# Rest of the modulation, first gelu and first layer norm beside the last gates instead of in the merge

## The chip, the cores and the metric

The kernel runs on one core of a Trainium2 chip. The metric is device time in microseconds of one execution. A core has TensorE (matrix products, an in-order queue of its own), VectorE, ScalarE and GpSimd, each with an in-order queue, and SyncE, which here issues most DMAs. TensorE's granted clock has the levels 1.2 and 2.4 GHz; the profile gives it as a share, 1.00 being the higher one.

## The reference

One layer of a hybrid backbone over 2048 latent tokens of 1024 channels with 256 context tokens. Cut to what the change touches:

```python
mod_l = silu_c @ ada_w + ada_b              # 1024 -> 6*1024, one row
sh1, sc1, g1, sh2, sc2, g2 = split(mod_l, 6)
zl = modulate(rmsnorm(x, norm1_g), sh1, sc1) @ w_in   # 512 | 1024 | 2048 columns
g  = gelu(s5_mixer(zl[:, :512]))
ya = (g * sigmoid(g @ w_glu)) @ w_a
yb = silu(layernorm(depthwise_conv1d(glu(zl[:, 512:1536])))) @ w_b
x  = x + g1 * ((sigmoid(ga) * ya + sigmoid(gb) * yb) @ w_out)   # ga, gb: zl[:, 1536:]
nl = modulate(rmsnorm(x, norm2_g), sh2, sc2)
x  = x + g2 * conv_ffn(nl)
```

Only `sh1` and `sc1` are needed for the first projection. The other four parts, `g1`, `sh2`, `sc2` and `g2` (4096 columns of `ada_w`), are needed after the merge.

## The kernel before, in words

Tokens lie on the free axis, in four blocks b = 0 to 3 of 512; channels lie on the 128 partitions. Each fp32 product is emulated by three matmuls of high and low halves (`mm3`, L462 to L464), so a 128-column tile of the projection with K = 1024 takes 24 matmuls of 128x512 for a block.

Order of the stages: a first phase (norm, modulation, the projection's S5 columns, the GLU columns), then 16 gate columns `gate(m)`, four blocks each, whose sigmoids (L859) go to DRAM. Beside the gate blocks `background()` advances two generators, the S5 scan and the depthwise convolution, both written to DRAM (`d_y`, `d_cv`). Gates m = 14 and 15 come last, in `last_gates`: block 3 of both, then blocks 0 to 2 of m = 14, then of m = 15.

The merge (`phase3a`) then runs over four blocks. In each it does 48 matmuls with `w_glu` on the gelu of the S5 output (`gh`, `go`), 96 with `w_b` on the layer-normed convolution (`sln`) and 96 with `w_a` (on `tgl`), multiplies by the stored gates and stores `mg`. While block b runs, `gelu_block(b + 1)` and `ln_block(b + 1)` prepare the next one. Gelu and layer norm of block 0 are emitted between the two halves of the last gates. The layer norm takes two sums over the channels by matmuls with ones: the mean (L977), after which the values are centred (L980) and squared, and the variance (L988), after which come L990 (variance), a square root on ScalarE, a reciprocal (L992), the products L993 to L996 and the product with the values (L998). The output is scaled and split into halves (L449 on ScalarE, L453 on VectorE).

The rest of the modulation (`ada_rest`) is a generator that the merge advances once per column m. For eight groups j of 512 columns and eight tiles k of 128 rows it loads 256 KB of `ada_w` (L924) into one of two slabs and adds it, times silu(c), to one of two accumulators (k = 0 by L926, the others by L928). `collect(j)` then sums the accumulator over the partitions: groups 0, 1, 6 and 7 (`g1`, `g2`) by one matmul L907 into a row, to which a bias row loaded into the tile `adrow` is added and which is stored to `d_row`; groups 2 to 5 (`sh2`, `sc2`) by four matmuls L913 into columns. In the text c0 to c7 are these collects.

A tile scheduler sets the order of each engine's queue from the program order and the priorities; `urgent()` raises that of the gates' sigmoids. Tiles come from pools: `z8` (8 buffers), `t16` (6), `raw` (3 landing buffers for weights), and two groups of PSUM tiles of four. Weight halves are loaded to `raw` and split by ScalarE (L449) and VectorE (L453).

Of the kernel before, what the change touches and what calls it, by code (L numbers as in the profile page):

```python
# [9 lines left out]
F32 = mybir.dt.float32  # L10
F32R = mybir.dt.float32r
# [12 lines left out]
T = 8  # L24
# [406 lines left out]
class Net:  # L431
# [6 lines left out]
    def __init__(self, nc, tc, ins, out):  # L438
        self.nc, self.tc, self.ins, self.out = nc, tc, ins, out
        self.v, self.a, self.g, self.pe = nc.vector, nc.scalar, nc.gpsimd, nc.tensor  # L440
        self.dma = nc.sync.dma_start
        self.store = nc.scalar.dma_start
        self.low = "g"


    def split(self, hi, lo, src, ha="a", la="v"):
# [150 lines left out]
    def phase1(self):  # L597
        nc, tc, ins, scr, v, a = self.nc, self.tc, self.ins, self.scr, self.v, self.a
        w_in = ins["w_in"]
        with ExitStack() as ctx:  # L600
# [152 lines left out]
            cvp = rx.enter_context(self.pool("cvp", 2, side="right"))  # L753
            fill = []

            stage = []

            def s5_all():
                yield from tabs
# [45 lines left out]
                    yield  # L805

            pace = [0.0, 0.0]

            def background(nconv=None, ns5=None):
# [80 lines left out]
            self.phase3a(last_gates(), lx, psum)  # L890


    def ada_rest(self, psum, fp):

        v, cp, pe = self.v, self.cp, self.pe
        self.A2 = cp.tile([128, 8], F32, name="A2")
# [4 lines left out]
        def collect(j, acc):  # L901
# [34 lines left out]
        v.scalar_tensor_tensor(self.A2, self.A2, 1.0, self.col["n2"], op0=OP.add, op1=OP.mult)  # L936
        yield

    def phase3a(self, last_gates, lx, psum):
        nc, tc, ins, scr, v, a, g_ = self.nc, self.tc, self.ins, self.scr, self.v, self.a, self.g  # L940
        with ExitStack() as ctx:
            fp = ctx.enter_context(self.pool("f3", 1, side="right"))
# [5 lines left out]
            def gelu_block(b):  # L948
                yr = self.z8("yr", [128, 4, T, 64])
                for ct in range(4):  # L950
                    self.dma(yr[:, ct], scr["y"][8 * ct:8 * ct + 8, :, :, 64 * b:64 * b + 64]
                             .rearrange("g h s c -> (g h) s c"))
                gl = self.z8("gl", [128, 4, 512])
                for ct in range(4):
                    a.activation(gl[:, ct].rearrange("p (c s) -> p c s", s=T),
                                 yr[:, ct].rearrange("p s c -> p c s"), AF.Gelu_apprx_tanh)
                gh = self.z8("gh", [128, 4, 512], F32R)
                go = self.z8("go", [128, 4, 512], F32R)
                for ct in range(4):
                    self.split(gh[:, ct], go[:, ct], gl[:, ct], "a", "v")  # L960
                return gl, gh, go

            def ln_block(b, out):

                t512 = lambda nm: fp.tile([128, 512], F32, name=nm, tag="ln", bufs=4)
                cv = self.z8("cv", [128, 4, 512])
                cb = lambda ct: self.col["cb"][:, ct:ct + 1]
                nb = 512 // CS
                for ct in range(4):
                    self.dma(cv[:, ct].rearrange("p (s x) -> p s x", s=CS), scr["cv"][ct][:, :, nb * b:nb * b + nb])  # L970
                s1, s2 = t512("s1"), t512("s2")
                v.scalar_tensor_tensor(s1, cv[:, 0], cb(0), cv[:, 1], op0=OP.add, op1=OP.add)
                v.scalar_tensor_tensor(s2, cv[:, 2], cb(2), cv[:, 3], op0=OP.add, op1=OP.add)
                v.scalar_tensor_tensor(s1, s1, self.cb13, s2, op0=OP.add, op1=OP.add)
                yield
                pm = psum.tile([128, 512], F32, name="ps", tag="ax")
                self.pe.matmul(pm, self.ones, s1, start=True, stop=True)  # L977
                a.activation(s2, pm, AF.Copy, scale=1.0 / D_CONV)
                for ct in range(4):
                    v.scalar_tensor_tensor(cv[:, ct], cv[:, ct], cb(ct), s2, op0=OP.add, op1=OP.subtract)  # L980
                q1, q2 = t512("q1"), t512("q2")
                a.activation(q1, cv[:, 0], AF.Square)
                for ct in range(1, 4):
                    a.activation(q2, cv[:, ct], AF.Square)
                    v.tensor_tensor(q1, q1, q2, op=OP.add)
                yield
                pv = psum.tile([128, 512], F32, name="ps", tag="ax")
                self.pe.matmul(pv, self.ones, q1, start=True, stop=True)  # L988
                va, sd, rs = t512("va"), t512("sd"), t512("rs")
                v.tensor_scalar(va, pv, 1.0 / D_CONV, EPS, op0=OP.mult, op1=OP.add)  # L990
                a.activation(sd, va, AF.Sqrt)
                v.reciprocal(rs, sd)  # L992
                v.tensor_tensor(sd, rs, rs, op=OP.mult)  # L993
                v.tensor_tensor(sd, sd, va, op=OP.mult)
                v.tensor_scalar(sd, sd, -0.5, 1.5, op0=OP.mult, op1=OP.add)
                v.tensor_tensor(rs, rs, sd, op=OP.mult)  # L996
                for ct in range(4):
                    v.tensor_tensor(cv[:, ct], cv[:, ct], rs, op=OP.mult)  # L998
                yield
                s = self.t16("sln", [128, 2, 4, 512])  # L1000
                out.append(s)
                for ct in range(4):
                    a.activation(cv[:, ct], cv[:, ct], AF.Silu, bias=self.col["lb"][:, ct:ct + 1],
                                 scale=self.col["lg"][:, ct:ct + 1])
                    nat = lambda z: z.rearrange("p (x s) -> p x s", s=CS)
                    self.split(nat(s[:, 0, ct]), nat(s[:, 1, ct]), cv[:, ct].rearrange("p (s x) -> p x s", s=CS), "a", "v")

            self.cb13 = self.cp.tile([128, 1], F32, name="cb13")
            v.tensor_tensor(self.cb13, self.col["cb"][:, 1:2], self.col["cb"][:, 3:4], op=OP.add)
            sq = []  # L1010
            next(last_gates)
            gnext = gelu_block(0)
            for _ in ln_block(0, sq):
                pass
            for _ in last_gates:
                pass
            lx.close()
            gp = ctx.enter_context(self.pool("g3", 3))
            wab = {}
            for nm, src in (("b", ins["w_b"]), ("a", ins["w_a"])):  # L1020
                for k2 in range(2):
                    wab[nm, k2] = self.t16(f"w{nm}{k2}", [128, 2, 2, 1024])
                for k in range(4):
                    for hf in range(2):
# [5 lines left out]
            self.wo = {}  # L1030
            for b in range(4):
                bs = slice(512 * b, 512 * b + 512)
                gl, gh, go = gnext
# [30 lines left out]
                for m in range(10):  # L1064
                    if m < 8:
                        wb(m)
                    if m == 1 and b < 3:
                        gnext = gelu_block(b + 1)
                    if m >= 2:
                        wa(m - 2)  # L1070
                    if m == 3 and b < 3:
                        ln = ln_block(b + 1, sq)
# [5 lines left out]
            for _ in ada:  # L1078
                pass


    def phase3b_4(self):
# [329 lines left out]
```

## Time and profile before

| | |
|---|---|
| median of 3 runs | 2810.7 us (2806.5 to 2811.0) |
| profiled execution | 2806.18 us, span 2804.4 us |
| TensorE busy | 2711.9 us, 97% of the span |
| VectorE busy | 1508.0 us, 54% |
| ScalarE busy | 822.7 us, 29% |
| gates 13 to 15 in the trace | 815.2 to 884.7 us |
| merge in the trace | 884.7 to 1147.7 us |

The span is the time from the first to the last instruction in the trace; the execution's own time is 1.8 us longer. In the rows PE is TensorE, PEld its weight loads, DVE VectorE, ACT ScalarE, POOL GpSimd, SP SyncE. "x2" behind a row means two instructions taken together, and a bracket behind a row gives the idle time of the engine before it and what ended it. Matmuls overlap with the next one, so a steady row of 0.39 us stands for a step of about 0.23 us from one start to the next.

### The profile page before, as it was taken

To read this page: it belongs to the slowest core of one execution; us is meant where nothing else is said; L and a number is where in the kernel's file an instruction comes from. 1 tells how busy PE (TensorE), PEld (TensorE's weight loads), DVE (VectorE), ACT (ScalarE), POOL (GpSimd) and SP (SyncE) were. 2 spreads that over 40 slices of the span, in tenths; PEclk is the share of its full clock that TensorE was granted. 3 is DMA by queue.
4 is the path that set the end of the run, shared out by engine and by line. 5 is a ranking of instruction groups with operands and counts; after the bars stand their busy time and mean duration, and the time that the engine had idled before them with its cause. 6 is when DMAs were issued, how large, how long until landed. Compare 5 with 4: busy or idle time off the path is not lost.

```text
span 2804.4 us, 32119 instructions
## 1 busy us (share of the span) xinstructions
PE 2711.9 (97%) x12044; PEld 2203.2 (79%) x12044; DVE 1508.0 (54%) x2312; ACT 822.7 (29%) x1446; POOL 459.3 (16%) x504
## 2 busy tenths in 40 slices
PE   7998999999999999999999999999999989999998
PEld 3786878788887777788888888888888878787887
DVE  5867643433316788566855646556465462414154
ACT  2555412121235443243421222212222132212122
POOL 2256477667600000000000000000000000000000
PEclk8999999999999999999999999999999999999999
DMA  8645745354436576533111111111111153323143
GB/s 315 195 142 165 205 138 153 126 177 147 145 102 202 173 206 200 187 131 113 64 46 57 42 49 49 49 53 46 45 57 42 53 179 107 113 71 135 53 143 98
DMA packets 327308, 334.73 MB, mean 119 GB/s; under 512 B 95336, under 2 KB 240360, under 8 KB 324464
## 3 DMA queue, kind: packets, MB, share of 16 engines
q1 hardware_dynamic: 245680, 235.13, 27.2%
q10 hardware_dynamic: 81472, 97.54, 10.0%
q8 instruction: 95, 1.56, 0.2%
q14 instruction: 61, 0.50, 0.1%
HBM read 230.38 MB, written 102.21 MB: 119 GB/s over the span
## 4 chain that ended last, share of the span: by engine, by line
PE 75%; DVE 9%; DMA 6%; POOL 5%; issue 2%; ACT 2%; SPq 0%; ACTq 0%; POOLq 0%; DVEq 0%
PE ps L464 23%; PE ps L462 23%; PE ps L463 23%; DMA sgab<-d_sg 2%; PE ps L795 1%; DVE Hs L408 1%; PE ps L577 1%; PE ps L385 1%; POOL t L395 1%; DVE Hs L410 1%; DMA slab<-in_ada_w_dram 1%; DMA ada<-in_ada_w_dram 1%; POOL t L394 1%; POOL t L361 1%; PE ps L1112 0%
## 5 line engine op out<-in xcount | busy, mean ns | idle before, releaser
L1242 DVE SCALAR_TENSOR_TENSOR acc<-pad,fw,acc 128x1024 f32<-128x1024 f32 x352 | 450.4, 1282 | 238.9 <-ACT acc L1238 229.5
L477 POOL TENSOR_TENSOR rs_y<-rs_v,mhalf 128x1 f32<-128x1 f32 (+1 forms) x41 | 27.4, 668 | 2048.8 <-DVE rs_v L476 2048.8
L462 PE MATMUL ps<-wd,hhl 128*128 128x512 f32 x704 | 275.6, 393 | 13.5 <-ACT hhl L449 7.3
L463 PE MATMUL ps<-wd,hhl 128*128 128x512 f32 x704 | 275.7, 392 | 0.0
L464 PE MATMUL ps<-wd,hhl 128*128 128x512 f32 x704 | 275.3, 392 | 0.1
L408 DVE TENSOR_TENSOR_SCAN Hs<-m,S 64x287 f32<-64x287 f32 x64 | 68.8, 1075 | 240.5 <-POOL S L396 240.1
L453 DVE TENSOR_TENSOR hhl<-hr,hhl 128x512 fp32r<-128x512 f32 (+1 forms) x110 | 63.0, 582 | 244.4 <-ACT hhl L449 244.1
L453 DVE TENSOR_TENSOR w_ch<-w_raw,w_ch 128x512 fp32r<-128x512 f32 x134 | 106.4, 801 | 137.9 <-ACT w_ch L449 137.5
L462 PEld LDWEIGHTS ps<-wd,hhl 128*128 128x128 f32 x704 | 133.2, 189 | 43.3 <-ACT hhl L449 7.9
L449 ACT CAST w_ch<-w_raw 128x512 fp32r<-128x512 f32 x142 | 87.6, 621 | 267.2 <-PE ps L464 167.1
L463 PEld LDWEIGHTS ps<-wd,hhl 128*128 128x128 f32 x704 | 133.2, 189 | 28.6 <-DVE wd L453 1.0
L464 PEld LDWEIGHTS ps<-wd,hhl 128*128 128x128 f32 x704 | 133.1, 189 | 28.5 <-DVE hhl L453 0.8
L449 ACT CAST hhl<-hr 128x512 fp32r<-128x512 f32 (+1 forms) x110 | 57.2, 534 | 264.5 <-PE ps L464 231.3
L463 PE MATMUL ps<-nm2l,w_ch 128*128 128x512 f32 x344 | 133.8, 389 | 0.0
L464 PE MATMUL ps<-nm2h,w_ch 128*128 128x512 f32 x344 | 133.8, 389 | 0.0
L462 PE MATMUL ps<-nm0h,w_ch 128*128 128x512 f32 x344 | 133.8, 389 | 0.0
L463 PE MATMUL ps<-nm0l,w_ch 128*128 128x512 f32 x344 | 133.8, 389 | 0.0
L463 PE MATMUL ps<-nm1l,w_ch 128*128 128x512 f32 x344 | 133.8, 389 | 0.0
L463 PE MATMUL ps<-nm3l,w_ch 128*128 128x512 f32 x344 | 133.8, 389 | 0.0
L464 PE MATMUL ps<-nm0h,w_ch 128*128 128x512 f32 x344 | 133.8, 389 | 0.0
L462 PE MATMUL ps<-nm1h,w_ch 128*128 128x512 f32 x344 | 133.8, 389 | 0.0
L464 PE MATMUL ps<-nm1h,w_ch 128*128 128x512 f32 x344 | 133.8, 389 | 0.0
(370 smaller groups left out, 6354.5 us busy)
## 6 DMA issues: line engine op xcount, KB each, us to landing
w_raw<-in_ffn_w_up_dram SPq DMA_DIRECT2D x88, 256.0 KB
d_hid<-acc ACTq DMA_DIRECT2D x88, 256.0 KB
w_raw<-in_ffn_w_down_dram SPq DMA_DIRECT2D x76, 256.0 KB
grp<-d_rec SPq DMA_DIRECT2D x32, 576.0 KB
hr<-d_hid SPq DMA_DIRECT2D x66, 256.0 KB
d_sg<-sgg ACTq DMA_DIRECT2D x64, 256.0 KB
ada<-in_ada_w_dram SPq DMA_DIRECT2D x64, 256.0 KB
sgab<-d_sg SPq DMA_DIRECT2D x32, 512.0 KB
```

The lines of the kernel that those rows point to most:

```text
L361: g_.tensor_tensor(r1, Hl, tb[:, 0:1, LAT].to_broadcast([128, 2, NCL]), op=OP.mult)
L385: nc.tensor.matmul(ps[:, :NX], sm[:, i, :], ug, start=True, stop=True)
L394: g_.tensor_tensor(t1, S, tb[:, 0:1, :].to_broadcast([128, 2, NX]), op=OP.mult)
L395: g_.tensor_tensor(t2, S[:, ::-1, :], tb[:, 1:2, :].to_broadcast([128, 2, NX]), op=OP.mult)
L408: v.tensor_tensor_scan(Hs[0:64, i, 1:1 + nsc], mb[0:64], S[0:64, i, 0:nsc], 0.0, op0=OP.mult, op1=OP.add)
L410: v.tensor_tensor_scan(Hs[64:128, i, NX - 1 - nsc:NX - 1][:, ::-1], mb[64:128], S[64:128, i, NX - nsc:NX][:, ::-1], 0.0, op0=OP.mult, op1= ...
L449: self.a.copy(hi, src)
L453: e.tensor_tensor(lo, src, hi.bitcast(F32), op=OP.subtract)
L462: mm(ps, wh, xh, start=first, stop=False)
L463: mm(ps, wh, xl, start=False, stop=False)
L464: mm(ps, wl, xh, start=False, stop=last)
L1242: v.scalar_tensor_tensor(acc[:, h], win(h, t // 3, t % 3), fw[:, i, t:t + 1], acc[:, h], op0=OP.mult, op1=OP.add)
```

## The change

The generator `before3a` takes `ada_rest`, the tile `cb13`, the gelu of block 0 and the three first steps of the layer norm of block 0 in this order. Once the S5 scan and the convolution are finished at the top of a gate from m = 12 on, the pool `f3` is opened and every further gate block advances `before3a` by two steps. The last gates go block by block, in the order 3, 2, 1, 0, with m = 14 and m = 15 in each. What is left of the generator, and the last step of the layer norm, run after the gates. The bias row of the L907 collects, L909 in the changed kernel, is now loaded into the accumulator's own first row instead of `adrow`. `gelu_block` and `ln_block` become methods with the same content.

```diff
@@ background, in the first phase
+                for _ in range(2):
+                    next(early3[0], None)
@@ the gates from m to 13
             while m < 14:
+                if not fill and next(s5, stage) is stage and not early:
+                    rx.close()
+                    early.append(self.phase3a_pool(rx))
+                    early3[0] = self.before3a(psum, early[0])
                 gate(m)
                 m += 1
-            while fill:
-                background(1, 0)
-            for _ in s5:
-                pass
-            rx.close()
+            assert early
@@ last_gates
-                for m in (14, 15):
-                    gate(m, (3,), w[m])
-                yield
-                for m in (14, 15):
-                    gate(m, (0, 1, 2), w[m])
+                for b in (3, 2, 1, 0):
+                    for m in (14, 15):
+                        gate(m, (b,), w[m])
+                    yield
@@ ada_rest, collect
-                row = fp.tile([1, 512], F32, name="adrow")
                 pe.matmul(ps[0:1, :], self.ones[:, 0:1], acc, start=True, stop=True)
+                row = acc[0:1, :]
@@ new
+    def before3a(self, psum, fp):
+        yield from self.ada_rest(psum)
+        self.cb13 = self.cp.tile([128, 1], F32, name="cb13")
+        self.v.tensor_tensor(self.cb13, self.col["cb"][:, 1:2], self.col["cb"][:, 3:4], op=OP.add)
+        self.g0 = self.gelu_block(0)
+        yield
+        self.ln0 = (self.ln_block(0, fp, psum, self.sq))
+        for _ in range(3):
+            next(self.ln0)
+            for _ in range(4):
+                yield
@@ phase3a
             next(last_gates)
-            gnext = gelu_block(0)
-            for _ in ln_block(0, sq):
-                pass
             for _ in last_gates:
                 pass
+            for _ in rest:
+                pass
+            for _ in self.ln0:
+                pass
+            sq, gnext = self.sq, self.g0
...
-            ada = self.ada_rest(psum, fp)
...
-                    next(ada, None)
```

The lines of the layer norm and the modulation have new numbers in the changed kernel: the mean L977 is L989, the centring L980 is L992, the variance L988 is L1000, the reciprocal L992 is L1004, the product L998 is L1010; L926 and L928 are L929 and L931, L907 and L913 are L909 and L916, and L462 to L464 are L463 to L465.

TensorE's queue in the kernel before, at the variance sum of the layer norm of block 0 (`q` is the sum of squares, `nl2h` and `nl2l` the normed input of token block 2, `w_ch` a gate's weights):

```order
L462 MATMUL ps<-nl2h,w_ch 128x512
L463 MATMUL ps<-nl2l,w_ch 128x512
L988 MATMUL ps<-q_6835,ones 128x512
L464 MATMUL ps<-nl2h,w_ch 128x512
L462 MATMUL ps<-nl2h,w_ch 128x512
L463 MATMUL ps<-nl2l,w_ch 128x512
```

TensorE's queue in the changed kernel, at the end of the gates (`gh` and `go` are the halves of the gelu, and the merge's first product begins with `gh`):

```order
L463 MATMUL ps<-nl0h,w_ch 128x512
L464 MATMUL ps<-nl0l,w_ch 128x512
L465 MATMUL ps<-nl0h,w_ch 128x512
L1000 MATMUL ps<-q_7179,ones 128x512
L909 MATMUL ps<-ada,ones 1x512 x2
L463 MATMUL ps<-gh,wglu_6785 128x512
L464 MATMUL ps<-go,wglu_6785 128x512
```

The variance sum stood among the gates, 80 matmuls ahead of the merge's first; now it is the first instruction behind the last gate, and the collects c6 and c7 stand between it and the merge.

VectorE's queue in the kernel before, from the variance of that layer norm on:

```order
L990 TENSOR_SCALAR va<-ps 128x512
L928 SCALAR_TENSOR_TENSOR ada<-ada,sc 128x512 x2
L992 RECIPROCAL rs<-sd 128x512
L928 SCALAR_TENSOR_TENSOR ada<-ada,sc 128x512
L993 TENSOR_TENSOR sd<-rs 128x512
L928 SCALAR_TENSOR_TENSOR ada<-ada,sc 128x512
L994 TENSOR_TENSOR sd<-sd,va 128x512
L995 TENSOR_SCALAR sd<-sd 128x512
L996 TENSOR_TENSOR rs<-rs,sd 128x512
L926 TENSOR_SCALAR ada<-ada,sc 128x512
L998 TENSOR_TENSOR cv<-cv,rs 128x512 x4
L928 SCALAR_TENSOR_TENSOR ada<-ada,sc 128x512 x2
```

The same place of VectorE's queue in the changed kernel, where the additions are those of group j = 7:

```order
L931 SCALAR_TENSOR_TENSOR ada<-ada,sc 128x512
L912 TENSOR_TENSOR ada<-ada,ps 1x512
L931 SCALAR_TENSOR_TENSOR ada<-ada,sc 128x512
L1005 TENSOR_TENSOR sd<-rs 128x512
L1006 TENSOR_TENSOR sd<-sd,va 128x512
L1007 TENSOR_SCALAR sd<-sd 128x512
L1008 TENSOR_TENSOR rs<-rs,sd 128x512
L931 SCALAR_TENSOR_TENSOR ada<-ada,sc 128x512
L1010 TENSOR_TENSOR cv<-cv,rs 128x512
L931 SCALAR_TENSOR_TENSOR ada<-ada,sc 128x512
L1010 TENSOR_TENSOR cv<-cv,rs 128x512 x3
L931 SCALAR_TENSOR_TENSOR ada<-ada,sc 128x512 x2
```

Before, the additions in this chain belonged to a group whose collect lies in the merge; now they belong to the group that c7 sums, and the last two of its eight stand behind the last product of the layer norm.

TensorE's queue in the changed kernel, at the mean of the layer norm (the matmuls behind it belong to the last two gate blocks, b = 0):

```order
L464 MATMUL ps<-nl1l,w_ch 128x512
L465 MATMUL ps<-nl1h,w_ch 128x512
L989 MATMUL ps<-s_7167,ones 128x512
L916 MATMUL ps<-ones,ada 128x1 x4
L463 MATMUL ps<-nl0h,w_ch 128x512
```

VectorE's queue there, from the two rows that make the sum for the mean on; the rows L931 from the first L992 on are the last three additions of group j = 5, which the four L916 sum:

```order
L985 SCALAR_TENSOR_TENSOR s_7168<-cv,cols 128x512
L986 SCALAR_TENSOR_TENSOR s_7167<-s_7167,cb_7140,s_7168 128x512
L931 SCALAR_TENSOR_TENSOR ada<-ada,sc 128x512 x2
L992 SCALAR_TENSOR_TENSOR cv<-cv,cols,s_7168 128x512
L931 SCALAR_TENSOR_TENSOR ada<-ada,sc 128x512
L992 SCALAR_TENSOR_TENSOR cv<-cv,cols,s_7168 128x512
L931 SCALAR_TENSOR_TENSOR ada<-ada,sc 128x512
L992 SCALAR_TENSOR_TENSOR cv<-cv,cols,s_7168 128x512 x2
L931 SCALAR_TENSOR_TENSOR ada<-ada,sc 128x512
```

The last addition of group 5 stands behind all four centring operations, which read the mean. In the kernel before no collect stood among the gates.

## Rows read from the trace of the kernel before

**Rows 1.** The page, busy time of each engine over the span.
```profile
PE 2711.9 (97%) x12044; PEld 2203.2 (79%) x12044; DVE 1508.0 (54%) x2312; ACT 822.7 (29%) x1446; POOL 459.3 (16%) x504
```

**Rows 2.** Busy time by stage: gates 13 to 15, and the merge.
```profile
core 0: us, PE busy (x) PEld busy (x) DVE busy (x) ACT busy (x) POOL busy (x), PEclk, DMA share, GB/s
815.20:884.70 69.50, 67.91 (x294) 54.60 (x293) 30.92 (x43) 25.34 (x37) 0.00 (x0) 1.00 0.50 144
884.70:1147.70 263.00, 246.29 (x1013) 192.35 (x1012) 205.63 (x309) 117.15 (x155) 0.00 (x0) 0.95 0.67 205
```

**Rows 3.** TensorE's waits, 765 to 1152 us: total us, times, longest.
```profile
PE ps L463 <- DVE sln L453: 3.5, 3, 2.2
PE ps L462 <- ACT wb L449: 3.4, 1, 3.4
PE ps L462 <- ACT sln L449: 2.6, 3, 0.9
...
PE ps L988 <- DVE q L985: 1.3, 1, 1.3
```

**Rows 4.** TensorE's timeline at two collects of the modulation (start, duration).
```profile
946.27 1.02 PE L907 MATMUL ps<-ada,ones 128*1 128x512 f32 x2
947.22 0.50 PE L462 MATMUL ps<-tgl,wa 128*128 128x512 f32 x1
...
1050.40 0.95 PE L913 MATMUL ps<-ones,ada 128*128 128x1 f32 x8
1051.21 0.49 PE L462 MATMUL ps<-sln,wb 128*128 128x512 f32 x1
```

**Rows 5.** The ada tile's operations: count, ns min/median/max, first and last start.
```profile
L928 DVE SCALAR_TENSOR_TENSOR ada<-ada,sc x56: 651/746/754, 857.6 to 1109.7; 128x512 f32<-128x512 f32 x56
L926 DVE TENSOR_SCALAR ada<-ada,sc x8: 470/480/487, 857.0 to 1088.0; 128x512 f32<-128x512 f32 x8
```

**Rows 6.** TensorE's timeline at the layer norm's sums and the merge's start.
```profile
857.18 1.12 PE L977 MATMUL ps<-s,ones 128*128 128x512 f32 x2 [0.40 <-DVE s L974]
857.74 0.79 PE L463 MATMUL ps<-nl1l,w_ch 128*128 128x512 f32 x1
...
865.88 1.02 PE L988 MATMUL ps<-q,ones 128*128 128x512 f32 x2
...
884.67 0.39 PE L462 MATMUL ps<-gh,wglu 128*128 128x512 f32 x1
```

**Rows 7.** VectorE's timeline of the layer norm of block 0.
```profile
858.98 2.74 DVE L980 SCALAR_TENSOR_TENSOR cv<-cv,cols,s 128x512 f32<-128x512 f32 x4 [0.67 <-ACT s L978]
...
866.95 0.69 DVE L990 TENSOR_SCALAR va<-ps 128x512 f32<-128x512 f32 x1 [0.82 <-PE ps L988]
...
870.02 3.35 DVE L992 RECIPROCAL rs<-sd 128x512 f32<-128x512 f32 x1
...
877.30 2.49 DVE L998 TENSOR_TENSOR cv<-cv,rs 128x512 f32<-128x512 f32 x4
```

**Rows 8.** The chain of waits, 855 to 890 us: loads of ada.
```profile
880.48 2.62 DMA ada<-in_ada_w_dram
...
884.79 3.63 DMA ada<-in_ada_w_dram
```

**Rows 9.** SyncE's timeline: issue of the layer norm's and the ada loads.
```profile
847.07 4.72 SPq L970 DMA_DIRECT2D cv<-d_cv  x4
...
859.36 30.31 SPq L924 DMA_DIRECT2D ada<-in_ada_w_dram  x15
```

**Rows 10.** ScalarE's timeline: sigmoids of two gate blocks in a row.
```profile
777.30 0.60 ACT L859 ACTIVATE sgg<-ps 128x512 f32<-128x512 f32 x1 [5.10 <-PE ps L464]
...
782.74 0.60 ACT L859 ACTIVATE sgg<-ps 128x512 f32<-128x512 f32 x1 [4.84 <-PE ps L464]
```

**Rows 11.** Busy time in two stretches of 10 us (columns as rows 2).
```profile
900.00:910.00 10.00, 8.89 (x27) 6.99 (x27) 6.86 (x11) 8.96 (x14) 0.00 (x0) 0.66 0.85 278
910.00:920.00 10.00, 7.83 (x27) 5.81 (x26) 8.43 (x15) 6.82 (x11) 0.00 (x0) 0.83 0.97 201
```

More of the change, by code (lines that the diff above doesn't have):

```diff
@@ L443, in __init__ @@
         self.low = "g"
+        self.sq = []
     def split(self, hi, lo, src, ha="a", la="v"):
@@ L754, in phase1 @@
             fill = []
-            stage = []
+            stage, early = [], []
             def s5_all():
@@ L807, in phase1 @@
             pace = [0.0, 0.0]
+            early3 = [iter(())]
             def background(nconv=None, ns5=None):
@@ L883, in last_gates, with ada_rest @@
                 w = {m: self.wtile(ring2, w_in, 1536 + 128 * m) for m in (14, 15)}
-                for m in (14, 15):
-                    gate(m, (3,), w[m])
-                yield
-                for m in (14, 15):
-                    gate(m, (0, 1, 2), w[m])
-            self.phase3a(last_gates(), lx, psum)
-    def ada_rest(self, psum, fp):
+                for b in (3, 2, 1, 0):
+                    for m in (14, 15):
+                        gate(m, (b,), w[m])
+                    yield
+            self.phase3a(last_gates(), early3[0], lx, rx, psum, early[0])
+    def ada_rest(self, psum):
         v, cp, pe = self.v, self.cp, self.pe
@@ L937, in ada_rest, with phase3a_pool @@
         yield
-    def phase3a(self, last_gates, lx, psum):
+    def phase3a_pool(self, stack):
+        return stack.enter_context(self.pool("f3", 1, side="right"))
+    def before3a(self, psum, fp):
[9 more added lines that the diff above has]
+                yield
@@ new lines, in gelu_block @@
+    def gelu_block(self, b):
+        scr, a = self.scr, self.a
+        yr = self.z8("yr", [128, 4, T, 64])
+        for ct in range(4):
+            self.dma(yr[:, ct], scr["y"][8 * ct:8 * ct + 8, :, :, 64 * b:64 * b + 64]
+                     .rearrange("g h s c -> (g h) s c"))
+        gl = self.z8("gl", [128, 4, 512])
+        for ct in range(4):
+            a.activation(gl[:, ct].rearrange("p (c s) -> p c s", s=T),
+                         yr[:, ct].rearrange("p s c -> p c s"), AF.Gelu_apprx_tanh)
+        gh = self.z8("gh", [128, 4, 512], F32R)
+        go = self.z8("go", [128, 4, 512], F32R)
+        for ct in range(4):
+            self.split(gh[:, ct], go[:, ct], gl[:, ct], "a", "v")
+        return gl, gh, go
@@ new lines, in ln_block @@
+    def ln_block(self, b, fp, psum, out):
+        v, a, scr = self.v, self.a, self.scr
+        t512 = lambda nm: fp.tile([128, 512], F32, name=nm, tag="ln", bufs=4)
+        cv = self.z8("cv", [128, 4, 512])
+        cb = lambda ct: self.col["cb"][:, ct:ct + 1]
+        nb = 512 // CS
+        for ct in range(4):
+            self.dma(cv[:, ct].rearrange("p (s x) -> p s x", s=CS), scr["cv"][ct][:, :, nb * b:nb * b + nb])
+        s1, s2 = t512("s1"), t512("s2")
+        v.scalar_tensor_tensor(s1, cv[:, 0], cb(0), cv[:, 1], op0=OP.add, op1=OP.add)
+        v.scalar_tensor_tensor(s2, cv[:, 2], cb(2), cv[:, 3], op0=OP.add, op1=OP.add)
+        v.scalar_tensor_tensor(s1, s1, self.cb13, s2, op0=OP.add, op1=OP.add)
+        yield
+        pm = psum.tile([128, 512], F32, name="ps", tag="ax")
+        self.pe.matmul(pm, self.ones, s1, start=True, stop=True)
+        a.activation(s2, pm, AF.Copy, scale=1.0 / D_CONV)
+        for ct in range(4):
+            v.scalar_tensor_tensor(cv[:, ct], cv[:, ct], cb(ct), s2, op0=OP.add, op1=OP.subtract)
+        q1, q2 = t512("q1"), t512("q2")
+        a.activation(q1, cv[:, 0], AF.Square)
+        for ct in range(1, 4):
+            a.activation(q2, cv[:, ct], AF.Square)
+            v.tensor_tensor(q1, q1, q2, op=OP.add)
+        yield
+        pv = psum.tile([128, 512], F32, name="ps", tag="ax")
+        self.pe.matmul(pv, self.ones, q1, start=True, stop=True)
+        va, sd, rs = t512("va"), t512("sd"), t512("rs")
+        v.tensor_scalar(va, pv, 1.0 / D_CONV, EPS, op0=OP.mult, op1=OP.add)
+        a.activation(sd, va, AF.Sqrt)
+        v.reciprocal(rs, sd)
+        v.tensor_tensor(sd, rs, rs, op=OP.mult)
+        v.tensor_tensor(sd, sd, va, op=OP.mult)
+        v.tensor_scalar(sd, sd, -0.5, 1.5, op0=OP.mult, op1=OP.add)
+        v.tensor_tensor(rs, rs, sd, op=OP.mult)
+        for ct in range(4):
+            v.tensor_tensor(cv[:, ct], cv[:, ct], rs, op=OP.mult)
+        yield
+        s = self.t16("sln", [128, 2, 4, 512])
+        out.append(s)
+        for ct in range(4):
+            a.activation(cv[:, ct], cv[:, ct], AF.Silu, bias=self.col["lb"][:, ct:ct + 1],
+                         scale=self.col["lg"][:, ct:ct + 1])
+            nat = lambda z: z.rearrange("p (x s) -> p x s", s=CS)
+            self.split(nat(s[:, 0, ct]), nat(s[:, 1, ct]), cv[:, ct].rearrange("p (s x) -> p x s", s=CS), "a", "v")
@@ L940, in phase3a @@
+    def phase3a(self, last_gates, rest, lx, rx, psum, fp):
         nc, tc, ins, scr, v, a, g_ = self.nc, self.tc, self.ins, self.scr, self.v, self.a, self.g
         with ExitStack() as ctx:
-            fp = ctx.enter_context(self.pool("f3", 1, side="right"))
+            ctx.push(rx)
             glu = [self.z8(f"wglu{q}", [128, 2, 2, 512], F32R) for q in range(2)]
@@ L946, in phase3a @@
             wglu = lambda k, ms: (glu[k // 2][:, k % 2, 0, ms], glu[k // 2][:, k % 2, 1, ms])
[L948 to L1006, printed above, removed]
@@ L1008, in phase3a @@
-            self.cb13 = self.cp.tile([128, 1], F32, name="cb13")
-            v.tensor_tensor(self.cb13, self.col["cb"][:, 1:2], self.col["cb"][:, 3:4], op=OP.add)
-            sq = []
             next(last_gates)
-            gnext = gelu_block(0)
-            for _ in ln_block(0, sq):
-                pass
             for _ in last_gates:
                 pass
+            for _ in rest:
[3 more added lines that the diff above has]
+            sq, gnext = self.sq, self.g0
@@ L1028, in phase3a @@
                                   wab[nm, k // 2][:, k % 2, 1, 128 * m:128 * m + 128]) for k in range(4)]
-            ada = self.ada_rest(psum, fp)
-            self.wo = {}
             for b in range(4):
@@ L1067, in phase3a @@
                     if m == 1 and b < 3:
-                        gnext = gelu_block(b + 1)
+                        gnext = self.gelu_block(b + 1)
                     if m >= 2:
@@ L1071, in phase3a @@
                     if m == 3 and b < 3:
-                        ln = ln_block(b + 1, sq)
+                        ln = self.ln_block(b + 1, fp, psum, sq)
                     if m % 2:
                         next(ln, None)
-                    next(ada, None)
                 for _ in ln:
                     pass
-            for _ in ada:
-                pass
     def phase3b_4(self):
```

## The prediction

> **What bounds the kernel now.** First the page's busy line: TensorE is busy for 97% of the span, VectorE for 54% [rows 1]. So the time is the length of TensorE's queue, and a change pays only where it takes matmuls or waits out of that queue. Second, the busy time by stage [rows 2]: during gates 13 to 15 TensorE idles for 69.50 − 67.91 = 1.6 us, and in the merge (884.70 to 1147.70) for 263.00 − 246.29 = 16.7 us. The merge's mean granted clock is 0.95, so 0.05 × 263 = 13 us more is lost there to the lower of the clock's levels, 1.2 instead of 2.4 GHz. Some 30 us of that stage are thus not matmuls at full speed: the upper limit of what relief of the merge could give. VectorE is busy for 205.6 of 263 us there (78%), against 30.9 of 69.5 (44%) in the gates. Third, TensorE's waits [rows 3]: no wait of the merge is on the modulation (ada). The long ones stand at the start of a block: the first w_b weights (3.4), the split of the layer norm's output (2.2 at the longest) and, once, the layer norm's variance sum L988 (1.3).
>
> **The change part by part.**
>
> *Modulation on TensorE.* Eight collects move from the merge to the gates. An L907 collect with its two neighbours takes 947.22 − 946.27 = 0.95 us, an L913 collect 1051.21 − 1050.40 = 0.81 [rows 4]; the matmul behind each lasts 0.50 and 0.49 instead of 0.39, which adds 0.1. That is 4 × 1.05 + 4 × 0.9 = 7.8 us into the gates and 7.8 us out of the merge: zero.
>
> *Modulation on VectorE.* 56 L928 at 0.746 and 8 L926 at 0.48 us [rows 5] are 45.6 us. VectorE stands idle for 38.6 us in the last 69.5 us of gates [rows 2], and more where gate 12's background has ended. They fit in sum; where they stand in the queue is what costs.
>
> *The new wait c5, behind the mean.* TensorE takes its queue strictly in order. In the changed kernel the collect of group j = 5 (c5) stands right behind L989, the layer norm's mean sum, and in front of the last pair of gate blocks. VectorE has the last three adds of that group behind the four centring operations, which need the mean. Before, the mean started at 857.18 [rows 6] and the centring at 858.98, 1.8 us later [rows 7]. So c5 comes 1.8 + 4 × 0.68 (2.74 for four) + 3 × 0.746 = 6.8 us after the mean's start, while TensorE is free 0.56 us after it (857.74): a wait of 6.2 us. Loads that lag make it longer, to some 10 us; the last add alone behind the centring is the lower end, 1.8 + 2.7 + 0.7 − 0.6 = 4.6 us. Nothing else on TensorE can pass: behind c5 are the 48 matmuls of two gate blocks.
>
> *The new wait c7, behind the variance.* This is the dearest term. Before, the variance sum started at 865.88 [rows 6] with gates behind it until 884.67, 18.8 us. Under them VectorE ran the chain: variance 866.95, reciprocal 870.02 (3.35 us), the products with the rstd at 877.30 for 2.49 us, to 879.79 [rows 7]. That chain took 879.79 − 865.88 = 13.9 us, held five ada operations (VectorE's order) and cost TensorE nothing. In the changed kernel the variance sum is the last thing before c6 and c7, and only the merge stands behind them. The eight ada operations of group 7 are threaded through this chain on VectorE, the last two behind the last product: 13.9 us, plus one ada operation and the collect's add more between (about 1.0), plus the two behind (1.5), makes 16.4 us after the variance's start. TensorE is free after the sum (1.0) and c6 (0.95), at 2.0: a wait of about 14.5 us. Lower end, with every load landed and the ada operations fitting between the chain's own waits: 13.9 − 5 × 0.7 + 1.5 − 2.0 = 10 us. Upper end, with the loads behind by a few of 2.0 us each: 20.
>
> *The loads, as a check.* The 64 loads pass through two slabs. The chain shows 2.6 to 3.6 us for one [rows 8]; with 2.75 us and 0.75 for the add, two slabs give one load per 1.75 us, and SyncE issued 15 in 30.31 us, 2.0 each [rows 9]. The change asks for four per gate block of 782.74 − 777.30 = 5.44 us [rows 10], 1.36 us each: more than the slabs carry, so the ada is paced by its loads. In gate 12 (21.8 us) some 12 to 14 go through; the other 50 to 52 take 88 to 104 us from 815.2 on, against 69.5 + 7.8 = 77.3 us of gates and collects. The shortfall, 10 to 27 us, has the size of the two waits (6.2 + 14.5 = 20.7).
>
> *Clock and weights.* In the merge the 10 us around the end of the 3.36 us wait (901.11) show clock 0.66, the next 10 us 0.83 [rows 11], so 3.4 and 1.7 us of full speed were lost. I take 2.5 us behind each of the two new waits, 5 in sum; bounds 0 and 10. The split of gate 14's weights stands behind an ada operation of 0.75 us once: 1 us.
>
> *What the merge gives back.* Beside the 7.8 us: the L988 wait (1.3) with about 2 us of clock, and 2 us at block 0, since three of w_b's eight halves load before the gates end. The other five stand on SyncE behind group 7's bias load, which waits for c7, so they gain nothing by the long wait. The starts of blocks 1 to 3 wait for the split of the layer norm's output, and ScalarE's and VectorE's order there stays: nothing. Together −5; bounds 0 and all 30 us.
>
> *Sum.* 7.8 + 6.2 + 14.5 + 5 + 1 = 34.5 in, 7.8 + 5 = 12.8 out: +21.7 us. Against the profiled execution (2806.2 us, span 2804.4) that is 2828. The median of the three runs is 4.5 us above the profiled one, and its highest 4.8; the spread alone could put the result at 2832. I stay at 2828, within 0.2% of both.
>
> **The rivals.** *Relief of the merge (not slower).* VectorE carries 45.6 us less in its fullest stage, so every block start could come earlier, and with the idle time the clock dips would go as well. For it: 78% VectorE, 16.7 us idle, the 13 us of clock. Against it: of the waits listed only L988's is one in which ada operations stand ahead. If all 30 us came back instead of 5, the sum is 2806.2 + 34.5 − 7.8 − 30 = 2803; if besides the two waits came out at their lower ends (4.6 and 10) and cost no clock, 2806.2 + 23.4 − 37.8 = 2792. It decides once the merge is shorter than 263 − 34.5 = 228.5 us. The Trainium skill states this rule (page "Perfetto Trace Analysis", section "Optimization Strategy"): where the most contended engine changes between regimes, interleaving them may help. Here TensorE is the fullest in both stages, so by the trace it bears on VectorE's part alone.
>
> *The stalls at their lower ends (no change).* c5 4.6, c7 10, clock 2, merge 15 beside the collects: 7.8 + 4.6 + 10 + 2 + 1 − 22.8 = +2.6, 2809, and 2816 if the merge gives 8. For it: what blocks 1 to 3 lose at their starts (the sln waits, 3.5 and 2.6 in sum [rows 3]) is work of VectorE and ScalarE, and VectorE has room now. Against it: the chain behind the variance is serial.
>
> *The ada late everywhere.* c3 and c4 stand behind the b = 3 and b = 2 pairs. SyncE issues gelu's and the layer norm's loads among the ada's, 4.7 us for four [rows 9]. With 52 loads at 2.0 and both groups, 104 + 9.4 = 113 us against 77.3: a shortfall of 36 us in place of 20.7, spread over c3, c4, c5 and c7, gives 2828 + 15 = 2843.
>
> *That the moved work is not done there* (the generator advanced late, the waits covered) is ruled out by the order of the instructions: all eight collects stand ahead of the merge's first matmul.
>
> **How the numbers follow.** A measurement of this kernel tells 0.2%, 5.6 us, from no change: 2805.1 to 2816.3 counts as the same. The forecast has a chance of 0.60, with its own range 2818 to 2838 (c7 from 12 to 17, clock 0 to 10, merge 0 to 10). The late ada has 0.17, the stalls at their lower ends 0.13, the relief 0.10. Slower by over 5.6 us is therefore 0.77, same 0.13, faster 0.10. The range that holds 8 in 10 leaves out the relief below 2805 and the longest late ada above 2845.
>
> **What would show it.** In the profile after: TensorE's waits list L909 and L916 on VectorE's ada, 14.5 us before the merge's first matmul and 6 us in front of the last gate pair; gelu's gemm starts 27 to 31 us later in the span than 884.67; the merge lasts about 250 us (263 − 7.8 − 5); a clock below 1.00 stands in the gates, where it was 1.00. The forecast is wrong if the wait ahead of the merge is under 8 us, or if the merge is under 235 us while the gates are as forecast.

## The result and the profile after

The changed kernel takes 2857.2 us (median of four runs, 2852.8 to 2860.7) against 2810.7: a ratio of 1.0165, 95% interval [1.0146, 1.0184], some 46 us slower. The forecast was slower, 2828 us; the time lies above its range. The profiled execution has a span of 2851.0 us, 46.6 more than before.

First the span is cut at four instructions of TensorE that stand in both traces: the last S5 product L368 (763.5 us before, 761.2 after), gate 11's first product (771.5, 779.5), the merge's first (884.7, 933.8) and the first of `wo` behind the merge (1147.7, 1191.1).

| us | before | after | difference |
|---|---|---|---|
| up to the last S5 product | 763.5 | 761.2 | −2.3 |
| S5 tail, to gate 11 | 8.0 | 18.3 | +10.3 |
| gates 11 to 15 | 113.1 | 154.3 | +41.2 |
| merge | 263.1 | 257.3 | −5.8 |
| behind the merge | 1656.7 | 1659.9 | +3.2 |

The windows of after for the S5 tail (from 1.4 us ahead of the last S5 product), gates 13 to 15 and the merge, to be read against [rows 2] (columns as there):

```profile
759.80:779.50 19.70, 12.06 (x55) 9.86 (x54) 8.26 (x12) 3.38 (x7) 5.19 (x4) 0.74 0.55 161
...
823.20:933.80 110.60, 81.91 (x333) 62.43 (x332) 58.49 (x86) 33.49 (x44) 0.00 (x0) 0.87 0.62 186
933.80:1191.10 257.30, 237.00 (x974) 185.78 (x973) 169.70 (x249) 112.75 (x151) 0.00 (x0) 0.96 0.51 149
```

TensorE idles for 7.6 us in the S5 tail and for 28.7 us in gates 13 to 15, at a clock of 0.87 there. In the merge VectorE's work fell from 205.6 to 169.7 us, yet TensorE still idles for 20.3 us there, more than the 16.7 of before. What VectorE was spared it spent waiting for `sgab`, the stored gates that the merge loads back into three buffers: 32.8 us in 20 waits before, and in after

```profile
  DMA sgab<-d_sg: 67.5, 19
```

TensorE's waits of after, 700 to 1200 us, say for what; they answer to [rows 3]:

```profile
PE ps L909 <- DVE ada L931: 17.9, 1, 17.9
PE ps L916 <- DVE ada L931: 10.0, 2, 6.1
PE ps L369 <- POOL S L363: 7.6, 1, 7.6
PE ps L463 <- ACT sln L450: 6.1, 4, 2.5
PE ps L1000 <- DVE q L997: 5.5, 3, 2.8
PE ps L463 <- DVE mg L1078: 4.2, 1, 4.2
```

The first two rows are c7, c5 (6.1) and c4 (4.0). The third is none that the forecast had. In the trace of before the last S5 scans on VectorE wait for GpSimd alone, and TensorE's last S5 products for nothing:

```profile
753.50 1.40 DVE L408 TENSOR_TENSOR_SCAN Hs<-m,S 64x287 f32<-64x287 f32 x1 [8.06 <-POOL S L396]
...
763.94 0.59 PE L369 MATMUL ps<-S,grp 128*128 128x256 f32 x2
```

The timeline of after over all engines shows the cause:

```profile
754.94 0.89 DVE L929 TENSOR_SCALAR ada<-ada,sc 128x512 f32<-128x512 f32 x1 [4.91 <-DMA ada<-in_ada_w_dram]
755.50 1.06 POOL L397 TENSOR_TENSOR S<-t,t 128x320 f32<-128x320 f32 x1
756.11 1.00 DVE L931 SCALAR_TENSOR_TENSOR ada<-ada,sc 128x512 f32<-128x512 f32 x1 [0.28 <-DMA ada<-in_ada_w_dram]
758.58 0.75 DVE L931 SCALAR_TENSOR_TENSOR ada<-ada,sc 128x512 f32<-128x512 f32 x1 [1.46 <-DMA ada<-in_ada_w_dram]
760.91 0.75 DVE L931 SCALAR_TENSOR_TENSOR ada<-ada,sc 128x512 f32<-128x512 f32 x1 [1.58 <-DMA ada<-in_ada_w_dram]
761.58 0.74 DVE L408 TENSOR_TENSOR_SCAN Hs<-m,S 64x287 f32<-64x287 f32 x1
...
764.75 1.76 POOL L361 TENSOR_TENSOR t<-Hs,grp 128x512 f32<-128x512 f32 x1 [8.19 <-DVE Hs L410]
...
769.40 1.22 PE L369 MATMUL ps<-S,grp 128*128 128x256 f32 x2 [7.63 <-POOL S L363]
```

Adds that wait for their loads stand in VectorE's queue ahead of the last S5 scans, whose input GpSimd had ready at 756.6; the scans begin at 761.58. GpSimd waits for the scan, and TensorE for GpSimd. SyncE's timeline of after shows why the modulation is late at the other end although it starts at 725 us:

```profile
725.31 7.79 SPq L927 DMA_DIRECT2D ada<-in_ada_w_dram  x4
...
735.82 1.31 SPq L927 DMA_DIRECT2D ada<-in_ada_w_dram  x2
...
744.26 2.03 SPq L927 DMA_DIRECT2D ada<-in_ada_w_dram  x2
...
749.68 17.74 SPq L927 DMA_DIRECT2D ada<-in_ada_w_dram  x8
...
770.04 1.13 SPq L927 DMA_DIRECT2D ada<-in_ada_w_dram  x2
...
824.28 0.27 SPq L911 DMA_DIRECT2D ada<-in_ada_b_dram  x1
...
826.80 0.24 SPq L913 DMA_DIRECT2D d_row<-ada  x1
828.55 4.75 SPq L927 DMA_DIRECT2D ada<-in_ada_w_dram  x4
```

TensorE's row for the first collect, c0:

```profile
823.23 1.02 PE L909 MATMUL ps<-ada,ones 128*1 128x512 f32 x2
```

After 18 loads none is issued from 772 to 828 us. Group 2 needs the accumulator of group 0, whose collect c0 stands behind eight gate blocks in TensorE's queue and runs at 823.2; then its bias row is loaded into that same accumulator, added and stored, 5.3 us more. The other 46 loads take from 828.55 to the last add at 931.15, 2.2 us each. The end of that, VectorE and then TensorE, answers to [rows 7] and [rows 6]:

```profile
913.28 0.69 DVE L1002 TENSOR_SCALAR va<-ps 128x512 f32<-128x512 f32 x1 [0.83 <-PE ps L1000]
...
921.83 0.75 DVE L931 SCALAR_TENSOR_TENSOR ada<-ada,sc 128x512 f32<-128x512 f32 x1 [1.01 <-DMA ada<-in_ada_w_dram]
...
926.07 0.75 DVE L931 SCALAR_TENSOR_TENSOR ada<-ada,sc 128x512 f32<-128x512 f32 x1 [0.98 <-DMA ada<-in_ada_w_dram]
...
928.14 1.89 DVE L1010 TENSOR_TENSOR cv<-cv,rs 128x512 f32<-128x512 f32 x3
...
931.15 0.75 DVE L931 SCALAR_TENSOR_TENSOR ada<-ada,sc 128x512 f32<-128x512 f32 x1 [0.46 <-DMA ada<-in_ada_w_dram]
```

```profile
932.05 1.86 PE L909 MATMUL ps<-ada,ones 128*1 128x512 f32 x2 [17.85 <-DVE ada L931]
```

Here both kinds of work hold each other up: the layer norm's chain waits for loads of the modulation, and the modulation's last adds stand behind the chain.

### The profile page after: what moved, and what is told of

Read it like the earlier page. It is cut to its first block, busy times and chain, and to the rows that moved or that the text cites. A ratio compares the mean times of both kernels' runs of the same rounds, so it can differ in the third digit from the quotient of the medians.

```text
span 2851.0 us, 32139 instructions
## 1 busy us (share of the span) xinstructions
PE 2717.6 (95%) x12044; PEld 2204.8 (77%) x12044; DVE 1517.4 (53%) x2312; ACT 817.4 (29%) x1442; POOL 462.9 (16%) x504
## 3 DMA queue, kind: packets, MB, share of 16 engines
q1 hardware_dynamic: 245680, 235.13, 27.2%
## 4 chain that ended last, share of the span: by engine, by line
PE 71%; DMA 8%; DVE 8%; POOL 5%; issue 3%; ACT 3%; SPq 0%; ACTq 0%; POOLq 0%; DVEq 0%
PE ps L465 22%; PE ps L463 22%; PE ps L464 22%; DMA sgab<-d_sg 3%; DMA ada<-in_ada_w_dram 2%; PE ps L796 1%; DVE Hs L408 1%; POOL t L395 1%; PE ps L385 1%; DVE Hs L410 1%; DMA w_raw<-in_w_in_dram 1%; POOL t L394 1%; POOL t L361 1%; POOL t L362 1%; ACT sln L450 1%
## 5 line engine op out<-in xcount | busy, mean ns | idle before, releaser
L463 PE MATMUL ps<-wd,hhl 128*128 128x512 f32 x704 | 275.7, 393 | 15.8 <-ACT hhl L450 8.6
L464 PE MATMUL ps<-wd,hhl 128*128 128x512 f32 x704 | 275.2, 391 | 0.0
L465 PE MATMUL ps<-wd,hhl 128*128 128x512 f32 x704 | 274.8, 391 | 0.1
L463 PEld LDWEIGHTS ps<-wd,hhl 128*128 128x128 f32 x704 | 133.0, 189 | 46.0 <-ACT hhl L450 9.4
L464 PEld LDWEIGHTS ps<-wd,hhl 128*128 128x128 f32 x704 | 133.1, 189 | 28.4 <-DVE wd L454 1.0
L465 PEld LDWEIGHTS ps<-wd,hhl 128*128 128x128 f32 x704 | 132.9, 189 | 28.2 <-DVE hhl L454 0.8
L463 PE MATMUL ps<-nm0h,w_ch 128*128 128x512 f32 x344 | 133.8, 389 | 0.0
L464 PE MATMUL ps<-nm0l,w_ch 128*128 128x512 f32 x344 | 133.8, 389 | 0.0
L465 PE MATMUL ps<-nm0h,w_ch 128*128 128x512 f32 x344 | 133.8, 389 | 0.0
L463 PE MATMUL ps<-nm1h,w_ch 128*128 128x512 f32 x344 | 133.8, 389 | 0.0
L464 PE MATMUL ps<-nm1l,w_ch 128*128 128x512 f32 x344 | 133.8, 389 | 0.0
L465 PE MATMUL ps<-nm1h,w_ch 128*128 128x512 f32 x344 | 133.8, 389 | 0.0
L463 PE MATMUL ps<-nm2h,w_ch 128*128 128x512 f32 x344 | 133.8, 389 | 0.0
L464 PE MATMUL ps<-nm2l,w_ch 128*128 128x512 f32 x344 | 133.8, 389 | 0.0
L465 PE MATMUL ps<-nm2h,w_ch 128*128 128x512 f32 x344 | 133.8, 389 | 0.0
L463 PE MATMUL ps<-nm3h,w_ch 128*128 128x512 f32 x344 | 133.8, 389 | 0.0
```

The source lines that it names most:

```text
L463: mm(ps, wh, xh, start=first, stop=False)
L464: mm(ps, wh, xl, start=False, stop=False)
L465: mm(ps, wl, xh, start=False, stop=last)
```

## The experiments

Each ratio is to the kernel before on the same chip. "Merge" is measured as in the table above.

**Without the modulation's loads and adds**, in the changed kernel (e1) and in the kernel before (e3):

```diff
-                self.dma(sl, self.ins["ada_w"][128 * k:128 * k + 128, c0:c0 + 512])
-                if k == 0: v.tensor_scalar(...)
-                else:      v.scalar_tensor_tensor(...)
+                if k == 0: v.memset(acc, 0.5)
```

> The changed kernel, but the 64 loads and 64 multiply-adds of the modulation are left out (the accumulators are filled with a constant, the eight collects stay). Theory A (the modulation's adds, late because their loads pause, cause the new waits at the S5 tail, c4, c5 and c7): the waits on ada (17.9 + 10.0 us) and the 7.6 us wait on the S5 sums vanish, and what is left is the first layer norm, whose mean now stands behind the last gate, some 13 to 17 us of wait ahead of the first w_b product: 2818 to 2832 us. Rival B (c7 waits for the layer norm's chain on VectorE, the modulation only stands in it): a wait of 14 us or more stays ahead of the merge's first product and the time stays at 2840 or more.

Measured: 2833.2 us, 1.0075 [1.0060, 1.0091], 1 us above A's range. The waits on ada and on the S5 sums are gone, 35.5 us in sum, and against the kernel before on the same chip the loss falls from 46 to 20 us. The merge starts at 893.0, with no wait ahead of it, but lasts 279.8 us. TensorE's timeline shows the layer norm's mean behind the last gate and what follows from it:

```profile
892.42 1.13 PE L986 MATMUL ps<-s,ones 128*128 128x512 f32 x2
...
917.73 2.07 PE L986 MATMUL ps<-s,ones 128*128 128x512 f32 x2 [11.81 <-DVE s L983]
...
925.68 0.80 PE L463 MATMUL ps<-sln,wb 128*128 128x512 f32 x1 [5.88 <-ACT wb L450]
```

The second L986 is the next block's mean, late behind the first block's chain. So A holds for the waits that it names. B's wait ahead of the merge is not there, but what B points at is: the layer norm is late in its own right, and the merge takes 17 us longer than before (279.8 against 263.1).

> The kernel before, but the 64 loads and 64 multiply-adds of the modulation are left out (constant accumulators, collects stay). Theory C (the merge's idle time comes from the loads of the gates and from the order of the next layer norm, not from VectorE's load): the merge stays within 8 us, 2799 to 2810 us. Rival D (VectorE's 45.6 us of modulation hold the merge): 20 to 30 us less, 2778 to 2790 us.

Measured: 2804.8 us, 0.9972 [0.9961, 0.9982], merge 254.6 us. Without loads and adds VectorE is busy for 175.7 us in the merge instead of 205.7: 30 us less, not 45.6, mainly since 12 of the 64 adds ran in the gates before and eight fills took the adds' place. That is worth 8 us in both numbers. Theory C holds, its 8 us for the merge exceeded by half a us: with three buffers for `sgab` that was about the most that relief of VectorE could have given. Run on the same chip as e1, e3 also gives the like-for-like price: without loads and adds on either side, the change still costs 2833.2 − 2804.8 = 28 us.

**Four accumulators** (e2):

```diff
+        accs += [fp.tile([128, 512], F32, name=f"acc{i}") for i in range(2)]
-            acc = accs[j % 2]
+            acc = accs[j % 4]
```

> The changed kernel with four accumulators instead of two. Theory A1 (no load was issued from 772 to 828 us because both accumulators waited for c0, which stands behind eight gate blocks on TensorE): the loads run on, the waits at c4, c5 and c7 vanish (27.9 us and some 6 us of clock), the S5 tail keeps its wait of about 8 us, and the layer norm's mean behind the gates costs 13 to 17 us ahead of the first w_b product: 2828 to 2842 us. Rival A2 (the loads' pace of 2.2 us each, or the chain on VectorE, sets c7): c7 still waits 10 us or more, 2850 or more.

Measured: 2844.2 us, 1.0116 [1.0100, 1.0132]. The loads run on in the former pause, no wait on ada is left, and the S5 tail keeps its 7.9 us. SyncE's and TensorE's rows:

```profile
783.42 21.48 SPq L928 DMA_DIRECT2D ada<-in_ada_w_dram  x11
```

```profile
927.60 2.08 PE L990 MATMUL ps<-s,ones 128*128 128x512 f32 x2 [12.22 <-DVE s L987]
```

The mechanism of A1 is shown, though the time lies 2 us above its range. 28 us of waits are gone and only 13 us gained: under them lay the late layer norm, as in e1 (merge 279.9).

**Bias row in a tile of its own** (e11), one part of the change undone:

```diff
-                row = acc[0:1, :]
+                row = fp.tile([1, 512], F32, name="adrow")
```

> The changed kernel with the bias row of four collects back in a tile of its own, so that the accumulator is free when TensorE has summed it. Theory A1 (after c0 the next add waits for bias load, add and store, 823.2 to 828.5 us, and 2 us again after c1): the loads restart some 4 us earlier and c7 comes 4 to 6 us earlier: 2849 to 2855 us. Rival G (the loads' pace takes the gain back): no change, 2855 to 2860 us.

Measured: 2840.5 us, 1.0098 [1.0081, 1.0115]. Gates 11 to 15 are 5.4 us shorter, as A1 says. But the merge is 8.4 and the part behind it 4.2 us shorter too, which no theory had and which puts the time 8.5 us below A1's range; the waits on the layer norm's variance fell from 5.5 to 1.4 us. That part stays open.

**Modulation's buffers in memory freed behind S5** (e6):

```diff
-        ar = Arena([self.z8("ada", [128, 2048])])
+        ar = Arena([fp.tile([128, 2048], F32, name="ada")])
```

> The changed kernel with the modulation's four buffers in the memory that is free only when the S5 scan and the convolution are done, so that no load or add can go ahead of the last scans. Theory A (the adds, waiting for their loads, stood ahead of the last S5 scan on VectorE): the 7.6 us wait on the S5 sums vanishes with its clock, the loads start 45 us later, but c0 stands at the same place and has its 16 loads by then, so the waits at c4 to c7 stay at 22 to 32 us in sum: 2838 to 2850 us. Rival E (the early loads are needed): c7 comes later by the 45 us, 2865 or more.

Measured: 2845.7 us, 1.0114 [1.0098, 1.0130]. The S5 tail is 8.0 us again. VectorE's last scan and first add:

```profile
757.44 0.75 DVE L410 TENSOR_TENSOR_SCAN Hs<-m,S 64x287 f32<-64x287 f32 x1
...
777.55 0.49 DVE L929 TENSOR_SCALAR ada<-ada,sc 128x512 f32<-128x512 f32 x1 [4.13 <-DMA ada<-in_ada_w_dram]
```

The collects still wait 27.2 us in sum (c7 18.0), since c0 stands where it stood. A is right in cause, and its range is met, but not by the sum that it names: gates 11 to 15 take 161.3 us instead of 154.3, with 5.4 us of waits on gate weights, so 7 of the 10 us come back, and most of the gain stands in the merge (248.6 us instead of 257.3), where no theory had it.

**Block order of the last gates alone** (e7), in the kernel before:

```diff
-                for m in (14, 15): gate(m, (3,), w[m])
-                yield
-                for m in (14, 15): gate(m, (0, 1, 2), w[m])
+                for b in (3, 2, 1, 0):
+                    for m in (14, 15): gate(m, (b,), w[m])
+                    yield
```

> The kernel before with the last two gate columns block by block (3, 2, 1, 0) and nothing else changed. All theories: no change, 2803 to 2815 us; the layer norm's variance still has some 79 matmuls behind it. Rival F (the new order of the gates itself puts the layer norm behind the gates): 2820 or more.

Measured: 2813.9 us, 1.0004 [0.9993, 1.0015]: no change. Yet the merge in its trace takes 268.1 us against 263.1 before. So a single trace tells little about a merge that is 5 us longer or shorter; where a ratio stands beside it, the ratio decides.

**Layer norm ahead of the second half of the modulation** (e5), and the same without loads and adds (e10):

```diff
-        yield from self.ada_rest(psum)
+        self.ada = self.ada_rest(psum, fp)
+        for _ in range(16):
+            next(self.ada)
+            yield
...
+                    next(ada, None)          # in the merge, per column, as before
```

> As the layer norm ahead of the second half of the modulation, but with the modulation's 64 loads and multiply-adds left out (constant accumulators, collects stay). Theory A (what the changed kernel still loses without loads is the place of the layer norm alone, and what is lost with the layer norm first is adds that wait for loads on VectorE in front of scans, weight splits and the mean): neither is left, 2797 to 2808 us. Rival B (the layer norm beside the gates costs by itself): 2815 or more.

Measured: 2814.8 us, 1.0003 [0.9993, 1.0012]. Against e1 18 us are gained, with the layer norm in its place (and five of the collects back in the merge), and no wait is left in the gates but 0.6 us on weights. But the time is above A's range and at the lower edge of B's: the merge takes 268.2 us, not the 254.6 of e3. Like for like, by the ratios of e10 and e3, some 9 us of the change's cost remain; they do not stand beside the gates, as B has it, and their cause is open.

> The changed kernel with another order in the generator: the modulation's first 16 of 36 steps, then gelu and layer norm of block 0, and the rest of the modulation step by step in the merge, as in the kernel before. Theory A (the generator holds more steps than the 16 gate blocks from gate 12 on can take, so modulation and layer norm both come late and each hides the other: taking out one alone leaves the other's wait): with the layer norm ahead both waits behind the gates vanish, the S5 tail keeps its 8 to 10 us, 2816 to 2824 us. Rival B (VectorE's load in the gates delays whatever stands there): the wait ahead of the merge or of its first w_b product stays over 8 us, 2830 or more.

Measured: 2838.0 us, 1.0088 [1.0073, 1.0104]. Behind the gates no wait on the modulation is left, as A says, but the time is over B's mark. Against e10 the loads and adds cost 23 us by the medians and 18 by the traces: 9 in the S5 tail and 9 in the gates, where the mean waits 4.3 us and weights 2.0. The mean's wait comes from another queue: SyncE issues the layer norm's own loads behind six of the modulation's, and VectorE idles 3.79 us for the last of them.

```profile
861.70 10.00 SPq L927 DMA_DIRECT2D ada<-in_ada_w_dram  x6
871.80 6.06 SPq L985 DMA_DIRECT2D cv<-d_cv  x4
```

My expectation had left out the gates.

**Slabs behind S5 and four accumulators** (e9):

```diff
+        accs = [ar(128, 512) for _ in range(4)]
+        slabs = [fp.tile([128, 512], F32, name=f"slab{i}") for i in range(2)]
```

> The changed kernel with the load slabs in memory freed behind S5 and with four accumulators, the layer norm still behind the modulation. Theory A (46 us are the S5 tail, about 10, the waits on the modulation net of what they hide, about 13, and the late layer norm under them, 20 to 25): the first two vanish, the third stays ahead of the merge or of its first w_b product: 2828 to 2838 us, as without any loads. Rival E (without early loads the modulation is late again): 2842 or more with waits on ada of over 10 us.

Measured: 2847.4 us, 1.0119 [1.0103, 1.0134]: A's sum fails. The S5 tail is mended (8.1 us), but the adds meet the next victim. TensorE's timeline:

```profile
852.32 0.80 PE L465 MATMUL ps<-nl3h,w_ch 128*128 128x512 f32 x1 [8.07 <-DVE w_ch L454]
...
911.47 1.86 PE L910 MATMUL ps<-ada,ones 128*1 128x512 f32 x2 [7.99 <-DVE ada L932]
```

The split of gate 14's weights now stands behind adds that wait for loads, as VectorE's rows show, and c7 still waits 8 us: E is half right.

```profile
850.91 0.75 DVE L932 SCALAR_TENSOR_TENSOR ada<-slab,sc,ada 128x512 f32<-128x512 f32 x1 [1.50 <-DMA slab<-in_ada_w_dram]
851.58 1.89 DVE L454 TENSOR_TENSOR w_ch<-w_raw,w_ch 128x512 fp32r<-128x512 f32 x3
```

**A fourth buffer for the gates read back** (e4), in the kernel before, and this with half of the modulation moved, layer norm first and slabs behind S5 (e8):

```diff
-                    sg = gp.tile([128, 2, 512], F32, name="sgab")
+                    sg = gp.tile([128, 2, 512], F32, name="sgab", bufs=4)
```

> The kernel before with four buffers instead of three for the gates that the merge loads back (sgab). Theory C (VectorE stands in front of late gate loads, 33 us in 20 waits, and holds up the layer norm behind them): the merge is 4 to 10 us shorter, 2797 to 2806 us. Rival D: no change, 2806 to 2811 us.

Measured: 2798.6 us, 0.9954 [0.9938, 0.9971], faster than both kernels. The merge's window, and what VectorE idled for ahead of work on `sgab` (32.8 us in 20 waits on the load before):

```profile
886.60:1140.00 253.40, 241.73 (x1014) 187.18 (x1012) 205.57 (x309) 117.69 (x156) 0.00 (x0) 0.98 0.72 216
```

```profile
  PE ps L464: 14.5, 13
  DMA sgab<-d_sg: 2.5, 3
```

VectorE does the same 205.6 us of work, in a merge 9.7 us shorter, at a clock of 0.98 instead of 0.95 [rows 2]. TensorE's waits on the split layer norm output fall from 6.1 to 2.1 us. C holds. The changed kernel with the fourth buffer alone was not run.

> The version to which the experiments point: as the layer norm ahead of the second half of the modulation, the load slabs in memory freed behind S5 (four accumulators), and four buffers for the gates loaded back. Theory A and C: no new wait is left, the S5 tail is as before, and the merge gains from the fourth buffer and from 24 adds less: 2792 to 2800 us. Rival D' (half of the modulation beside the gates still costs there): 2803 or more, more than the fourth buffer alone.

Measured: 2817.7 us, 1.0021 [1.0011, 1.0031]; D' holds. The same wait on gate 14's weights is there (8.5 us), and in the merge the next layer norm's mean waits 4.3 us. Moving half of the modulation loses 19 us against e4.

## Why the prediction was right in sign and wrong in size

- *c5, 6.2 us*: right, 6.05. *Collects, zero net*: nothing contradicts it. *Clock, 5 us*: about right; gates 11 to 15 grew by 41.2 us, of which collects 7.8 and waits 28.7 − 1.6 leave 6.3.
- *c7, 14.5 us*: 17.85. The place was right, the cause only in part. I took the chain of the layer norm as given and the adds as threaded through it; in the trace the chain itself waited for loads. And c7's wait was no price of its own: e2 takes it away and the late layer norm shows in its place.
- *The step that failed: "the loads, as a check", and with it the place of the adds (next point).* I let 12 to 14 loads go in gate 12 and the rest run from 815 us on. In the trace 18 went before gate 11, and none for 56 us after. The accumulators' reuse behind c0 [e2], and the bias row in them [e11], were not in the working. The other 46 loads took 103 us; my figure for the remaining 50 to 52 was 88 to 104.
- *"They fit in sum; where they stand in the queue is what costs"*: I looked at VectorE's queue from gate 13 on only. The adds are also ahead of the last S5 scans: 10.3 us, the largest part of the miss, for which the sum had no term [e1, e6, e9].
- *What the merge gives back, 12.8 us*: 5.8. The 7.8 us of collects left it, but TensorE's waits grew instead of shrinking: on the variance from 1.3 to 5.5 us, on `mg` from 2.5 to 4.2, while the 3.4 on w_b's weights went. Relief by VectorE was rightly priced low: without all loads and adds it is 8 us [e3]. A third or more of the some 30 us in the merge was the price of one missing buffer for the gates read back: 10 us in the trace, 13 by the ratio [e4]. I had not seen it, though VectorE's idle time named it.
- *Rivals.* "The ada late everywhere" came nearest: c4 did wait, 4.0 us, and c3 did not. Its 15 us were too few since it, too, began at gate 13. Relief, and stalls at their lower ends, did not occur. Relief also counted 45.6 us of adds out of the merge, where only 36.5 lay: the first adds stand at 857 us [rows 5], ahead of the merge's start.

The ledger against the forecast's +21.7 us, profile against profile: S5 tail +10.3, merge +7.0, c4 +4.0, c7 +3.4, behind the merge +3.2, c5, clock and weights −0.7, the start −2.3, which makes the 46.6 measured. By knocking out, like for like: of the 46 us, 28 remain when neither kernel has loads and adds (e1 and e3), and 9 when the layer norm also comes first (e10 and e3). So 18 us go with the moved loads and adds, 19 with the late layer norm, and 9 have no shown cause.

Open: why the merge took 268 us in e10 and 255 in e3 with like work, and 249 in e6 and e11; and the 3.2 us behind the merge. In the twelve traces other than that of before that last part, whose program is nearly the same, took 1655.7 to 1662.3 us, so a single trace decides nothing below some 6 us there; by e7 the merge's terms in the ledger are no surer than 5 us.

## What to carry to other kernels

Work moved to an idle engine is not hidden by that idle time: what waits for a load in an in-order queue delays everything behind it (scans, a weight split, and on SyncE another load), so look at each instruction that another engine waits for and ask what now stands ahead of it, from where the scheduler may first place the moved work and not from where the text emits it. A result that is collected by a busy engine keeps its buffers until that engine's queue gets there; count buffers against that depth. When two waits end at one place, taking out one shows only the difference: test both alone and together.

## What the runs showed that was not expected

VectorE's 78% in the merge was not its limit: with 30 us less of its work there the merge fell by 8 us [e3], with one more 512 KB buffer and the same work by 10 [e4]. Spared work came back as waiting: in the changed kernel VectorE has 36 us less to do in the merge and idles 35 us longer for the same loads. Where TensorE's waits went, its clock came back as well: 0.95 to 0.98 in e4.
